# An encoder layer on one core: early feed-forward weights loaded three pairs ahead into other buffers, ten early pairs in place of nine, two of them ahead of the second normalisation

## The chip, the core and the metric

One Trainium2 chip, one core of it. TensorE (PE in the profile) multiplies matrices, with a row of its own for loading the stationary operand (PEld); VectorE (DVE), ScalarE (ACT) and GpSimd (POOL) do the element-wise work; SyncE (SP) issues most transfers. Each engine takes its instructions strictly in the order in which they were written into its queue. The metric is the device time of one execution in microseconds (us), lower is better. A measurement of this kernel is the median of several runs.

## The reference, cut to what matters

One layer over 1024 tokens of width 1024, in float32, with an input normalisation, three kinds of attention, and a feed-forward part of width 4096:

```
x    = layer_norm(x, ln_in_g, ln_in_b)
proj = x @ w_in                                  # heads A, B and C
mix  = concat(A(proj), B(proj), C(proj)) @ w_out
x    = layer_norm(alpha * x + mix, ln_mix_g, ln_mix_b)
hdn  = relu(x @ w_ff1)
x    = layer_norm(alpha * x + (hdn * hdn) @ w_ff2, ln_ff_g, ln_ff_b)
```

## The kernel before, in words

Every matrix product is made of float32 operands split into a high and a low part (a cast on ACT, then a subtraction on DVE; `split`, lines 825 and 826), and three matmuls for each pair of blocks. The two feed-forward products go through a scheme with seven products for a 2 x 2 block product (Strassen and Winograd), numbered m = 1 to 7.

**The stretch of the change** is the passage from the mixing to the first feed-forward product. The tokens are worked on in two halves of 512. `out_ab(t)` (line 792) multiplies the heads of token block t with w_out and adds the result to a running sum; `out_ab(7)` is the last. `ln_mix_half(0)` normalises token blocks 0 to 3 while the last blocks of the attention are still under way; its four pieces make the operands `xo[1]` and `xo[2]`, which are all that the products m = 1 and m = 2 need. `ln_mix_half(1)` needs `out_ab(7)`. It has four pieces too, and each makes, for one k, the operands of m = 6, 7, 5, 4 and 3: eight transposes (line 872), two activations (line 873), four differences, five splits.

**Early pairs.** The columns of w_ff1 are taken in 16 pairs of 128-column blocks, j = 0 to 15. For the first `N_EARLY` = 9 of them, m = 1 and m = 2 are done ahead of the main loop, so that TensorE has something to do while the second half is being normalised. An early pair costs one load of 512 KB (`w1_early`, line 917), two splits of two halves each, 24 matmuls of 512 columns into the PSUM tiles `psS` (line 953), a copy and a sum, a squared relu, and two stores to DRAM (`dd`, `hd`), from which the main loop reads them back. The load goes into the buffer `raw`, of which there is one, so the load of pair j + 1 can begin only when both halves of pair j have been split. `EARLY_LN` = 1 of these pairs stands ahead of `ln_mix_half(1)` in the program; the other eight stand behind its pieces, two to each piece, and their matmuls are queued behind the last transpose that was written before that piece (`after`).

**The main loop** goes through the remaining (j, m), five steps (m = 6, 7, 5, 4, 3) for an early pair and seven for another, with operands prepared five steps ahead by `w1_prep` (line 924). It loads the pair's whole 1 MB of w_ff1 into a buffer `w1r` of the tag `tab`, of which there are two. During the mixing the two `tab` buffers hold two of w_out's blocks (`hd`; `load_wout(0)` and `load_wout(1)`). The second feed-forward product follows.

Operands live in *pages* (36 buffers of 4 KB a partition, tag `pg`), given out in the program's order. A planner decides the order of instructions on each engine ahead of time, by the program's order, by priorities (`high_priority`), by its own estimate of times, and by `issue_after`, which queues what a block writes for an instruction's engine behind that instruction. Once decided, the order doesn't change on the chip.

Of the kernel before, what the change touches and what calls it, by code (L numbers as in the profile page):

```python
# [10 lines left out]
F32 = mybir.dt.float32  # L11
# [6 lines left out]
P = 128  # L18
# [35 lines left out]
LN_MIX_AT, LN_MIX_PER = 64, 2  # L54


N_EARLY, EARLY_LN = 9, 1
NORM_FIRST = 120
AHEAD, AHEAD2 = 5, 4
ROWS_AT, C_AT, LAST_STEPS = 28, 6, 8  # L60
# [17 lines left out]
def encoder_kernel(ctx: ExitStack, tc: tile.TileContext, A: dict, out: bass.AP):  # L78
    nc = tc.nc

    sb = ctx.enter_context(tc.tile_pool(name="sb", bufs=1))
# [5 lines left out]
    def nm(p):  # L87
        cnt[0] += 1
        return f"{p}_{cnt[0]}"

    def page(shape, dt=F32):
        return sb.tile(shape, dt, tag="pg", bufs=N_PG, name=nm("pg"))
# [16 lines left out]
    def ps_mm():  # L109
        return ps.tile([P, 512], F32, tag="mm", bufs=NM, name=nm("psm"))  # L110
# [13 lines left out]
    def load(out, in_):  # L124
        last_load[0] = nc.sync.dma_start(out=out, in_=in_)
# [6 lines left out]
    def half_sl(h):  # L132
        return slice(h * 512, h * 512 + 512)
# [4 lines left out]
    def mm3(o, pairs):  # L138

        n = 3 * len(pairs)  # L140
        i = 0
        for (ah, al, bh, bl) in pairs:
            for a, b in ((ah, bh), (ah, bl), (al, bh)):
                nc.tensor.matmul(o, a, b, start=(i == 0), stop=(i == n - 1))  # L144
                i += 1

# [14 lines left out]
    def w_cols(w, c0, n, k0=0, nk=8):  # L163
        return w[k0 * P:(k0 + nk) * P, c0:c0 + n].rearrange("(k p) c -> p k c", p=P)
# [162 lines left out]
    def mm_feat(w, half):  # L327
        pm = ps_mm()
        mm3(pm, [(w[0][:, k, :], w[1][:, k, :], xT[half][k][:, 0, :], xT[half][k][:, 1, :]) for k in range(8)])
        return pm  # L330
# [56 lines left out]
    def proj_tok(t, ws, dest, pm):  # L387
        xt = xT[t // 4]
        sl = slice((t % 4) * P, (t % 4) * P + P)
        mm3(pm[:, 0:256], [(xt[k][:, 0, sl], xt[k][:, 1, sl], ws[k // 4][0][:, k % 4, :], ws[k // 4][1][:, k % 4, :])  # L390
                           for k in range(8)])
        n = 4 // len(dest)
        for j, d in enumerate(dest):
            pv = pm[:, 64 * n * j:64 * n * (j + 1)].rearrange("p (h d) -> p h d", h=n)
            nc.scalar.copy(out=d[:, :, 0:64], in_=pv)
            sub(d[:, :, 64:128], pv, f32(d[:, :, 0:64]))
# [370 lines left out]
    w_out = A["w_out"]  # L767

    w_o = {}

    def load_wout(c, paged):
        dest = None
        if c < 2:
            dest = hd_tab()
        elif paged:
            dest = page([P, D], F32R), page([P, D], F32R)
        w_o[c] = split_w(w_out[c * P:(c + 1) * P, :], [P, D], dest, page([P, D]) if paged else None, pool=True)

    def heads_of(t, n):
        return [o[:, t * P:(t + 1) * P] for o in o_ca[n]]  # L780

    def out_c(t):

        for nh in range(2):
            pm = ps_mm()
            sl = half_sl(nh)
            mm3(pm, [(*heads_of(t, n), w_o[6 + n][0][:, sl], w_o[6 + n][1][:, sl]) for n in range(2)])
            a_t = evb([P, 512])
            nc.scalar.copy(out=a_t, in_=pm)
            nc.gpsimd.dma_start(out=y1[t][:, sl], in_=a_t, accum_op=ALU.add)  # L790

    def out_ab(t, ob):

        a_t = page([P, D])
        load(out=a_t, in_=y1[t])
        for nh in range(2):
            pm = ps_mm()
            sl = half_sl(nh)
            mm3(pm, [(*heads_of(t, 2 + n), w_o[n][0][:, sl], w_o[n][1][:, sl]) for n in range(2)]
                + [(ob[:, 0, n], ob[:, 1, n], w_o[2 + n][0][:, sl], w_o[2 + n][1][:, sl]) for n in range(4)])  # L800
            nc.vector.tensor_tensor(out=a_t[:, sl], in0=a_t[:, sl], in1=pm, op=ALU.add)
        return a_t
# [6 lines left out]
    w_ff1, w_ff2 = A["w_ff1"], A["w_ff2"]  # L809
# [7 lines left out]
    def tab8(shape, name):  # L817
        return sb.tile(shape, F32, tag="tab", bufs=2, name=nm(name))
# [4 lines left out]
    def split(pg, x):  # L823

        nc.scalar.copy(out=pg[:, 0], in_=x)  # L825
        last_split[0] = nc.vector.tensor_tensor(out=pg[:, 1], in0=x, in1=f32(pg[:, 0]), op=ALU.subtract)  # L826
# [86 lines left out]
    def w1_split(j, m, x):  # L913
        w1op[j, m] = page([P, 2, 4, P], F32R)
        split(w1op[j, m], x)

    def w1_early(j):

        w = sb.tile([P, 8, P], F32, tag="raw", bufs=1, name=nm("w1e"))
        load(out=w, in_=w_cols(w_ff1, 256 * j, P))  # L920
        for c in range(2):
            w1_split(j, 1 + c, w[:, 4 * c:4 * c + 4])

    def w1_prep(j, m):

# [305 lines left out]
    for n in range(64 + B_VALUES):  # L1231
# [20 lines left out]
        for _ in range(2):  # L1252
            m = a_done[0]
            if m < 16 and n > 31 + C_VALUES and n >= 32 + m + A_VALUES:
                h, b = divmod(m, 4)
# [7 lines left out]
        if m >= 0:  # L1263
            t, g = divmod(m, 2)
            if g == 0:
                oTb[t] = page([P, 2, 4, P], F32R)
            b_values(t, g, b_rt.pop(m), b_vs, oTb[t])
            if g == 1:
                with tc.high_priority(offset=-(OUT_OFF if t < NT - 1 else 0)):
                    fa[t] = out_ab(t, oTb.pop(t))  # L1270
# [11 lines left out]

    early = range(N_EARLY)

    def ahead(j, after=None):
        if j + 1 < N_EARLY:
            w1_early(j + 1)
        with (tc.issue_after(after.ins) if after else ExitStack()):
            ff1(j, 1, True)
            ff1(j, 2, True)  # L1290

    w1_early(0)
    for j in early[:EARLY_LN]:
        ahead(j)
    pieces = ln_mix_half(1)
    rest = list(early[EARLY_LN:])
    for k in range(4):
        after = last_tr[0]
        pieces[k]()
        for j in rest[k * len(rest) // 4:(k + 1) * len(rest) // 4]:  # L1300
            ahead(j, after)
# [138 lines left out]
```

## Time and profile before

| | |
|---|---|
| median of three runs | 1206.79 us (1206.04 to 1209.1) |
| profiled execution | 1206.19 us, of which 1204.4 us are the span of the trace |
| mean granted TensorE clock over the span | 0.986 |
| PE, PEld busy | 1143.8 us, 946.1 us of the span |
| DVE, ACT, POOL busy | 956.2 us, 641.3 us, 413.4 us |

Times in the rows are microseconds from the start of the span. A matmul's record is longer than its pace, since matmuls are pipelined: one of 512 columns is recorded with 0.39 us. The chain of waits gives the pace, since there each piece ends where the next begins. An idle time stands in brackets with what ended it.

### The profile page before, as it was taken

The numbers are of one execution on the slowest core, as the hardware profiler recorded it, in microseconds if no ns is written. First come the engines' busy times: TensorE is split into PE (matmuls) and PEld (weight loads), VectorE is DVE, ScalarE is ACT, GpSimd is POOL, SyncE is SP. The second block draws the span as 40 slices with busy tenths as digits, with TensorE's granted clock in tenths as the row PEclk, the third lists the DMA queues.
The fourth block names the chain that finished last, engine by engine and source line by source line (L and its number), as shares of the span: only waits on it lengthen the run. The fifth ranks groups of instructions, "written<-read, shape, count | busy, mean of one in ns | idle before, by whom it ended". The sixth has DMA issues, their size and how long they took to land.

```text
span 1204.4 us, 17122 instructions
## 1 busy us (share of the span) xinstructions
PE 1143.8 (95%) x5642; PEld 946.1 (79%) x5642; DVE 956.2 (79%) x1858; ACT 641.3 (53%) x1253; POOL 413.4 (34%) x367
## 2 busy tenths in 40 slices
PE   4999999999988989998799999999999999999997
PEld 3788789878877868876568888888888888888885
DVE  8556999998666598876569989988884997787985
ACT  4534667666556877755564544545553444444530
POOL 4775656775666865320011222221210000000201
PEclk8999999999999999999899999999999999999998
DMA  8566844364769962224355678665599655355631
GB/s 275 190 235 186 280 135 144 114 161 135 233 195 282 190 144 88 63 79 149 100 171 199 229 258 283 237 236 199 174 345 367 225 182 183 95 175 186 227 123 70
DMA packets 138000, 227.15 MB, mean 189 GB/s; under 512 B 11820, under 2 KB 75212, under 8 KB 137912
## 3 DMA queue, kind: packets, MB, share of 16 engines
q1 hardware_dynamic: 122472, 177.55, 46.9%
q0 software_dynamic: 15440, 48.51, 11.7%
q8 instruction: 45, 0.74, 0.3%
q14 instruction: 43, 0.35, 0.1%
HBM read 156.49 MB, written 77.34 MB: 194 GB/s over the span
## 4 chain that ended last, share of the span: by engine, by line
PE 72%; DVE 8%; ACT 4%; issue 3%; DMA 3%; POOL 1%; SPq 0%; DVEq 0%; ACTq 0%; POOLq 0%
PE psm L144 13%; PE psS L1083 11%; PE psS L953 8%; PE pst L953 7%; PE psm L953 7%; PE psm L1083 5%; PE pst L1083 5%; PE pspv L1083 4%; DMA w1e<-in_w_ff 2%; PE pspv L514 2%; PE pst L499 2%; PE psS L470 2%; DVE pg L473 1%; DVE pg L130 1%; DVE pg L826 1%
## 5 line engine op out<-in xcount | busy, mean ns | idle before, releaser
L144 PE MATMUL psm<-pg,whi 128*128 128x512 f32 x448 | 152.7, 406 | 2.1 <-DVE pg L245 1.8
L953 PE MATMUL psS<-pg,pg 128*128 128x512 f32 x576 | 139.9, 396 | 8.2 <-ACT pg L825 5.2
L217 POOL TENSOR_TENSOR bnve<-bnve,pw 128x1 f32<-128x1 f32 x24 | 22.5, 939 | 357.5 <-DVE bnve L216 355.3
L1083 PE MATMUL psS<-pg,pg 128*128 128x512 f32 x576 | 140.4, 389 | 0.0
L953 PEld LDWEIGHTS psS<-pg,pg 128*128 128x128 f32 x576 | 108.2, 190 | 35.0 <-ACT pg L825 8.4
L1083 PEld LDWEIGHTS psS<-pg,pg 128*128 128x128 f32 x576 | 108.1, 188 | 22.4
L825 ACT CAST pg<-hr 128x512 fp32r<-128x512 f32 x112 | 69.3, 619 | 97.5 <-PE pst L1083 39.5
L477 ACT ACTIVATE pg<-pg,cst 128x1024 f32<-128x1024 f32 x64 | 73.8, 1154 | 51.6 <-DVE cst L473 48.6
L144 PEld LDWEIGHTS psm<-pg,whi 128*128 128x128 f32 x448 | 83.7, 191 | 21.7 <-DVE pg L245 2.2
L144 PE MATMUL psm<-pg,wlo 128*128 128x512 f32 x224 | 89.3, 399 | 0.8 <-POOL wlo L160 0.8
L953 PE MATMUL psm<-pg,pg 128*128 128x512 f32 x384 | 89.8, 389 | 0.0
L953 PE MATMUL pst<-pg,pg 128*128 128x512 f32 x384 | 89.6, 389 | 0.0
L826 DVE TENSOR_TENSOR pg<-hr,pg 128x512 fp32r<-128x512 f32 x112 | 76.7, 685 | 13.6 <-ACT pg L825 13.4
L953 PEld LDWEIGHTS pst<-pg,pg 128*128 128x128 f32 x384 | 72.1, 188 | 15.0
L953 PEld LDWEIGHTS psm<-pg,pg 128*128 128x128 f32 x384 | 72.1, 188 | 15.0
L130 DVE TENSOR_TENSOR pg<-pst,pg 128x512 fp32r<-128x512 f32 (+2 forms) x112 | 65.0, 589 | 22.2 <-ACT pg L639 8.1
L484 POOL TENSOR_TENSOR pg<-pg,cst 128x704 f32<-128x704 f32 x32 | 49.2, 1536 | 80.1 <-DVE cst L481 57.7
L1083 PE MATMUL psm<-pg,pg 128*128 128x512 f32 x288 | 74.2, 389 | 0.0
L1083 PE MATMUL pst<-pg,pg 128*128 128x512 f32 x288 | 74.2, 389 | 0.0
L144 PE MATMUL psm<-whi,pg 128*128 128x256 f32 (+1 forms) x256 | 72.4, 349 | 1.0 <-DVE pg L130 0.7
L961 POOL DMA_DIRECT2D hd<-evb x80 | 43.2, 540 | 85.6 <-DVE evb L821 80.9
L964 ACT ACTIVATE h<-h 128x512 f32<-128x512 f32 x55 | 34.5, 631 | 71.1 <-DVE h L821 71.0
(208 smaller groups left out, 2769.2 us busy)
## 6 DMA issues: line engine op xcount, KB each, us to landing
hr<-hd SPq DMA_DIRECT2D x28, 1024.0 KB, 5.7
hd<-evb POOLq DMA_DIRECT2D x80, 256.0 KB, 4.1
w1r<-in_w_ff SPq DMA_DIRECT2D x16, 1024.0 KB, 5.4
evb<-in_w_ff SPq DMA_DIRECT2D x64, 256.0 KB, 3.6
qk<-evb SPq DMA_DIRECT2D x52, 256.0 KB, 4.2
y<-pg POOLq DMA_DIRECT2D x24, 512.0 KB, 4.7
pg<-y SPq DMA_DIRECT2D x24, 512.0 KB, 9.2
pg<-in_w_ff SPq DMA_DIRECT2D x32, 256.0 KB, 6.0
```

The costliest lines, as they stand in the source:

```text
L130: nc.vector.tensor_tensor(out=o, in0=a, in1=b, op=ALU.subtract)
L144: nc.tensor.matmul(o, a, b, start=(i == 0), stop=(i == n - 1))
L470: last_mm[0] = nc.tensor.matmul(sc, q[:, m, (i % 2) * P:(i % 2) * P + P], kst[h][kh][:, m, :], start=True, stop=True)
L477: nc.scalar.activation(out=rt, in_=rt, func=AF.Exp, scale=-1.0, bias=sm[:, m:m + 1], accum_out=sm[:, 2 + m:3 + m])
L484: nc.gpsimd.tensor_tensor(out=R[1][:, a], in0=R[1][:, a], in1=sm[:, 6:7].broadcast_to([P, C_POOL]), op=ALU.mult)
L499: nc.tensor.transpose(pt[:, kb * P:(kb + 1) * P], src[:, c0:c0 + P], ident)
L825: nc.scalar.copy(out=pg[:, 0], in_=x)
L826: last_split[0] = nc.vector.tensor_tensor(out=pg[:, 1], in0=x, in1=f32(pg[:, 0]), op=ALU.subtract)
L953: nc.tensor.matmul(o, w[:, e, k], xo[m][k][:, f], start=(n == 0), stop=(n == 11))
L961: nc.gpsimd.dma_start(out=hd_d[m - 1, j], in_=x)
L964: nc.scalar.activation(out=dst, in_=dst, func=AF.Relu)
L1083: nc.tensor.matmul(o, h[:, e, sl], w[:, f], start=(k == 0 and n == 0), stop=(k == 15 and n == 2))
```

## The change

The loading of an early pair's weights is taken out of `w1_early` and becomes `w1_early_load`. It runs three pairs ahead: pairs 0, 1 and 2 are loaded before the first split, and pair j + 3 is loaded when pair j is worked on. Pair 0 still goes into `raw`, pairs 1 and 2 into a page each, and pairs 3 to 9 into the two `tab` buffers, from which the mixing's w_out blocks have gone and into which `w1_prep` loads afterwards. There are ten early pairs, not nine, and two of them, not one, ahead of `ln_mix_half(1)`. The matmuls of these two are now queued behind the last matmul of `out_ab(7)` (`last_ab`, which `mm3` returns); before, the one such pair had no such tie.

```diff
--- before.py
+++ after.py
@@ -54,7 +54,7 @@
 LN_MIX_AT, LN_MIX_PER = 64, 2
 
 
-N_EARLY, EARLY_LN = 9, 1
+N_EARLY, EARLY_LN = 10, 2
 NORM_FIRST = 120
 AHEAD, AHEAD2 = 5, 4
 ROWS_AT, C_AT, LAST_STEPS = 28, 6, 8
@@ -141,8 +141,9 @@
         i = 0
         for (ah, al, bh, bl) in pairs:
             for a, b in ((ah, bh), (ah, bl), (al, bh)):
-                nc.tensor.matmul(o, a, b, start=(i == 0), stop=(i == n - 1))
+                mm = nc.tensor.matmul(o, a, b, start=(i == 0), stop=(i == n - 1))
                 i += 1
+        return mm
 
 
 
@@ -767,6 +768,7 @@
     w_out = A["w_out"]
 
     w_o = {}
+    last_ab = [None]
 
     def load_wout(c, paged):
         dest = None
@@ -796,7 +798,7 @@
         for nh in range(2):
             pm = ps_mm()
             sl = half_sl(nh)
-            mm3(pm, [(*heads_of(t, 2 + n), w_o[n][0][:, sl], w_o[n][1][:, sl]) for n in range(2)]
+            last_ab[0] = mm3(pm, [(*heads_of(t, 2 + n), w_o[n][0][:, sl], w_o[n][1][:, sl]) for n in range(2)]
                 + [(ob[:, 0, n], ob[:, 1, n], w_o[2 + n][0][:, sl], w_o[2 + n][1][:, sl]) for n in range(4)])
             nc.vector.tensor_tensor(out=a_t[:, sl], in0=a_t[:, sl], in1=pm, op=ALU.add)
         return a_t
@@ -914,12 +916,24 @@
         w1op[j, m] = page([P, 2, 4, P], F32R)
         split(w1op[j, m], x)
 
+    w1e = {}
+
+    def w1_early_load(j):
+
+        if j >= N_EARLY:
+            return
+        if j == 0:
+            w1e[j] = sb.tile([P, 8, P], F32, tag="raw", bufs=1, name=nm("w1e"))
+        else:
+            w1e[j] = page([P, 8, P]) if j < 3 else tab8([P, 8, P], "w1e")
+        load(out=w1e[j], in_=w_cols(w_ff1, 256 * j, P))
+
     def w1_early(j):
 
-        w = sb.tile([P, 8, P], F32, tag="raw", bufs=1, name=nm("w1e"))
-        load(out=w, in_=w_cols(w_ff1, 256 * j, P))
-        for c in range(2):
-            w1_split(j, 1 + c, w[:, 4 * c:4 * c + 4])
+        if j < N_EARLY:
+            w = w1e.pop(j)
+            for c in range(2):
+                w1_split(j, 1 + c, w[:, 4 * c:4 * c + 4])
 
     def w1_prep(j, m):
 
@@ -1282,16 +1296,19 @@
 
     early = range(N_EARLY)
 
-    def ahead(j, after=None):
-        if j + 1 < N_EARLY:
-            w1_early(j + 1)
-        with (tc.issue_after(after.ins) if after else ExitStack()):
+    def ahead(j, after):
+
+        w1_early_load(j + 3)
+        w1_early(j + 1)
+        with tc.issue_after(after.ins):
             ff1(j, 1, True)
             ff1(j, 2, True)
 
+    for j in range(3):
+        w1_early_load(j)
     w1_early(0)
     for j in early[:EARLY_LN]:
-        ahead(j)
+        ahead(j, last_ab[0])
     pieces = ln_mix_half(1)
     rest = list(early[EARLY_LN:])
     for k in range(4):
```

## Rows read from the trace of the kernel before

**Rows 1.** Windows: busy time (count) of each engine, granted clock, DMA share, GB/s.

```profile
558.19:629.42 71.23, 58.43 (x244) 44.29 (x242) 41.50 (x70) 39.34 (x71) 9.24 (x17) 0.95 0.49 157
...
570.00:580.00 10.00, 5.98 (x19) 4.81 (x20) 4.75 (x9) 4.00 (x6) 1.70 (x3) 0.66 0.43 142
...
630.00:1100.00 470.00, 470.00 (x2075) 389.17 (x2075) 394.49 (x628) 219.09 (x384) 61.48 (x114) 1.00 0.65 224
```

**Rows 2.** The chain that ended last, 559 to 643 us: start, duration, what.

```profile
559.65 6.11 DMA w1e<-in_w_ff
...
576.67 6.00 PE psS L953 x19
...
582.68 0.45 PE pst L872 x4
...
588.83 0.60 DVE evb L130
...
624.37 4.36 DMA w1e<-in_w_ff
...
637.95 5.44 PE psm L953 x24
```

**Rows 3.** TensorE in order of time: start, duration, work, [idle before, releaser].

```profile
559.58 2.00 PE L144 MATMUL psm<-pg,pg 128*128 128x512 f32 x8
...
561.41 4.02 PE L953 MATMUL psS<-pg,pg 128*128 128x512 f32 x17
...
565.26 0.40 PE L144 MATMUL psm<-whi,pg 128*128 128x512 f32 x1
...
568.97 0.40 PE L144 MATMUL psm<-whi,pg 128*128 128x512 f32 x1
...
573.36 0.69 PE L872 MATMUL pst<-ident,pg 128*128 128x128 f32 x2 [3.99 <-DVE pg L862]
...
574.71 1.97 PE L872 MATMUL pst<-ident,pg 128*128 128x128 f32 x8 [0.66 <-ACT pg L873]
...
587.15 1.25 PE L953 MATMUL psS<-pg,pg 128*128 128x512 f32 x4 [2.00 <-ACT pg L825]
...
590.09 4.87 PE L953 MATMUL psS<-pg,pg 128*128 128x512 f32 x20 [1.08 <-DVE pg L826]
...
629.42 8.53 PE L953 MATMUL psS<-pg,pg 128*128 128x512 f32 x36 [1.15 <-ACT pg L825]
```

**Rows 4.** DVE in order of time, same columns.

```profile
560.69 0.87 DVE L130 TENSOR_TENSOR pg<-evb,pg 64x256 fp32r<-64x256 f32 x2 [0.47 <-ACT pg L762]
...
567.71 0.68 DVE L801 TENSOR_TENSOR pg<-pg,psm 128x512 f32<-128x512 f32 x1
...
631.33 0.69 DVE L821 TENSOR_TENSOR w1t<-w1r 128x512 f32<-128x512 f32 x1
...
634.13 0.69 DVE L826 TENSOR_TENSOR pg<-w1t,pg 128x512 fp32r<-128x512 f32 x1 [1.39 <-ACT pg L825]
```

**Rows 5.** ACT in order of time, same columns.

```profile
583.89 2.17 ACT L825 CAST pg<-evb 128x512 fp32r<-128x512 f32 x4
...
586.48 1.14 ACT L825 CAST pg<-w1e 128x512 fp32r<-128x512 f32 x2
```

**Rows 6.** Waits of ACT from 569.3 to 629.5 us: total, times, longest.

```profile
ACT pg L825 <- DMA w1e<-in_w_ff: 10.8, 6, 5.5
```

**Rows 7.** SP's queue in order of time, same columns as rows 3.

```profile
552.95 1.08 SPq L125 DMA_DIRECT2D w1r<-in_w_ff  x2
...
554.20 1.26 SPq L125 DMA_DIRECT2D pg<-y  x1
```

**Rows 8.** DMA issues, 400 to 660 us: count, KB each, us to landing.

```profile
w1r<-in_w_ff SPq DMA_DIRECT2D x5, 1024.0 KB, 5.4
...
w1e<-in_w_ff SPq DMA_DIRECT2D x9, 512.0 KB, 4.0
...
pg<-y SPq DMA_DIRECT2D x8, 512.0 KB, 9.5
```

## The prediction, made blind

> **What bounds the kernel now.** I read the windows first, to find where TensorE is not full; then the chain of waits and TensorE in order of time through that place; then DVE, ACT and SP there, to see what each gap waits for.
>
> From 630 us on TensorE is busy without a gap (470.00 of 470.00 us, clock 1.00) [rows 1]. So whatever makes the main loop begin earlier brings the end earlier by as much. From 558.19 to 629.42 it is not full. The pace is 24 matmuls in 5.44 us, 0.227 us each, and four transposes in 0.45 us [rows 2]. The stretch holds 24 matmuls of `out_ab(7)`, 192 of the first eight early pairs (by the code; the block of 36 at 629.42 is the ninth pair's 24 and the main loop's first 12) and 32 transposes: 216 x 0.227 + 32 x 0.11 = 52.5 us in 71.2 us. **18.7 us are lost there.** In four places [rows 2, 3]:
> - 568.97 to 576.67: 4.0 us without any work until the last token block is normalised, then transposes that wait on ACT. Some 6 us.
> - 576.67 to 582.68: 19 matmuls take 6.00 us where 4.3 are due. TensorE's clock was granted at 0.66 of 2.4 GHz over 570 to 580 [rows 1], so part of it ran at 1.2 GHz, after that idle stretch. 1.7 us.
> - 582.68 to 590.09: 9 matmuls and 16 transposes (3.8 us) in 7.4 us. The gap of 2.0 us ends with a split on ACT, and the split of the early weights (586.48) stands behind four casts of the normalisation (583.89) [rows 5]. Its load was not late; its place in ACT's order was. 3.6 us.
> - 590.09 to 629.42: 140 matmuls, 31.7 us, in 39.3 us. 7.6 us. The chain shows the load of the early weights five times (first 6.11, last 4.36 us) [rows 2], and ACT's casts wait 10.8 us for these loads [rows 6]. One buffer, a load of 4.0 us [rows 8] and a split make a cycle longer than the 5.44 us of matmuls that it feeds.
>
> By PE's busy time alone (58.43 of 71.23 [rows 1]) only 12.8 us would be lost. The Trainium skill says in "Perfetto Trace Analysis", section "Identifying the Most-Contended Engine", that matmul busy time is a poor measure, since matmuls are pipelined, and that the busy share of weight loads is a better one. By that measure PEld's 44.29 us at the 0.828 of the full stretch (389.17 of 470.00) are 53.5 us of work and 17.7 us lost. The trace agrees: a count by pace gives 18.7. By busy time the sum below would end about 6 us higher.
>
> **The change part by part.**
>
> *Pairs 0 and 1 behind `out_ab(7)`.* Now 17 matmuls of pair 0 run between the two parts of `out_ab(7)` (561.41 to 565.26), more are mixed into the second part, and its last starts at 568.97 [rows 3]. Without them: 12 matmuls from 558.19 to 560.9; the operand of the other 12 is ready at 560.69 + 0.87 = 561.56 [rows 4]; 12 x 0.227 = 2.7, end at 564.3. If the second part starts no earlier than now (565.26), it ends at 568.0. I take 564.3, as the operand allows it; bounds 0 and 3.7 us later.
>
> *What the normalisation's gap then holds.* From the last matmul to the first dependent transpose there are 4.4 us (568.97 to 573.36). Two pairs are 10.9 us of work and cover it with 6.5 us to spare, so the gap and the slow clock behind it are gone: cost 0, and 6 + 1.7 us if that cover fails.
>
> *Ten pairs with loads ahead.* From 564.3: 240 x 0.227 + 32 x 0.11 = 58.0, so the main loop could begin at 622.3. Now it begins at 629.42 + 5.44 = 634.86, with one pair (5.44 us) more left in it. Ceiling: 634.86 + 5.44 - 622.3 = **18.0 us**.
>
> *What is kept of the stalls.* The 16 transposes ahead of pair 2 go through two banks that ACT empties: 573.36 to 576.67 is 3.3 us for at most 1.8 of work. Minus 1.5 (bounds 0 and 2.2). ACT's order: pair 2's split is now written ahead of the second normalisation, the later ones not. I keep half of 3.6: minus 1.8 (bounds 0 and 3.6). Load waits: a load is due two pairs after its issue, 10.9 us against 4.0 alone and, for several together, the 9.5 us of the y load issued right behind two large ones [rows 7, 8]: 0 (bound 2).
>
> *The main loop's weights.* `w1r` for pairs 0 and 1 is now loaded at 552.95 [rows 7], long before its use at 631.33 [rows 4]. The early pairs take those buffers, so it comes after the split of pair 8. Then 5.4 us of load [rows 8] and 3.5 us of preparation (631.33 to 634.13 + 0.69) are 8.9 us, against 10.9 us of matmuls of pairs 8 and 9 if that split is done as pair 8 starts. Minus 1 (bounds 0 and 3).
>
> *At no cost.* SP: pairs 3 and 4 take the place of the two `w1r` loads in its queue. Behind these stands the sum's load (554.20); 9.5 us later it is there at 563.7, the first sum could start at about 563, and a microsecond there stays under the 6.5 us of cover. The tenth pair adds one load, two stores and two loads back, and SP and POOL are mostly idle here. DVE and ACT have 41.50 and 39.34 us of work in the 71.2 us [rows 1]; with the tenth pair's share (three DVE instructions of 0.60 us [rows 2], two casts and three activations on ACT of about as much each) that fits into 64. Its splits leave the main loop, where DVE has 394.49 of 470 us busy and TensorE stays full. Two pages more are taken, shortly before `out_ab(7)` gives back eight (four of heads, four of weights); without that cover the two loads start 5 us later and still come before pair 1 is due at 569.7.
>
> Sum: 18.0 - 1.5 - 1.8 - 1.0 = 13.7 us. The profiled execution took 1206.19 us, 0.6 below the median: 1206.19 - 13.7 = **1192.5 us**.
>
> **The rivals.** Three microseconds and a half (0.3%) are what a measurement here tells from no change.
> - *Order, not loads, sets the pace* (0.20). Only the last part's 7.6 us come back, since transposes and splits stay as tangled in the planned order as now: 1198.6, within 1197 to 1203. For it: DVE waits on ACT and ACT on transposes between 577 and 587. Against: two pairs written and split ahead of the tangle.
> - *One wait for another* (0.10). The loads now wait for pages or for `tab` buffers, and what the early pairs gain the main loop loses on `w1r`: 7.6 + 6 gained at most, 3.7 lost at `out_ab(7)`, up to 8.9 at `w1r` if the split of pair 8 is as late as pair 9. That leaves a gain of 1.0, 1205.2, within 1203 to 1208. Against: 10.9 us of matmuls between.
> - *Slower* (0.13). Pair 0 is no longer there to fill TensorE while the last attention block is finished. The fill is 3.85 us (561.41 to 565.26), and a gap of that length was followed by 1.7 us of slow clock: 5.6 us. If ACT's place in the order, and not the loads, is what holds the pairs, so that less than 5.6 us come back, the kernel is slower, up to 1211.8. Against: the operand is there at 561.56, and ACT waited 10.8 us on loads.
>
> **How the numbers follow.** Forecast 0.57, by itself 1188 (all 18.0 us) to 1198 (stalls at their bounds, 2.2 + 3.6 + 2 + 2). With the first rival and part of the second, 1188 to 1204 holds eight in ten. Faster: 0.57 + 0.20 + 0.03 = 0.80; the same 0.07; slower 0.13 with the slow edge of the second rival in it.
>
> **What would show it.** Right: no wait of ACT on `w1e` loads, no `w1e` in the chain, the clock near 1.00 through 570 to 580, `out_ab(7)` ending near 564, the main loop's first `psS` matmuls near 626, `w1r` issued about 610. Wrong, if TensorE is empty between 561 and 565 for long, if the first main step waits for `w1r`, or if the gaps before early matmuls stay and name ACT's casts with loads long landed: then the order, and not the loads, was the pace.

## The result, and the profile after

The changed kernel took 1192.43 us (median of four runs, 1191.89 to 1196.56), the kernel before 1206.41 us over its four runs. The ratio is 0.9893, 95% interval 0.986 to 0.9926: 0.7 to 1.4% faster, clear of the 0.3% within which two times can't be told apart here. 1192.5 us were forecast. The profiled execution has a span of 1190.4 us where it was 1204.4.

The windows of the kernel after, with the columns of [rows 1]. The first stretch goes from the same place, the 12 matmuls of `out_ab(7)` on pages, to the main loop's first step:

```profile
557.89:626.53 68.64, 65.85 (x292) 53.23 (x291) 46.75 (x78) 43.96 (x80) 11.41 (x21) 0.98 0.59 191
...
570.00:580.00 10.00, 9.70 (x48) 7.61 (x47) 4.59 (x7) 6.16 (x10) 2.74 (x5) 1.00 0.42 157
...
586.00:590.00 4.00, 3.92 (x12) 3.06 (x13) 4.00 (x8) 4.00 (x9) 0.00 (x0) 0.57 0.00 0
...
630.00:1080.00 450.00, 450.00 (x1987) 372.63 (x1986) 381.60 (x608) 209.34 (x365) 59.86 (x111) 1.00 0.67 230
```

TensorE is still full from 630 us on, so the whole difference lies ahead of it. Before, that stretch held nine pairs and lasted from 558.19 to 634.86, 76.7 us; now it holds ten and lasts 68.6. With 5.44 us for the tenth pair that is 13.5 us, and the span is 14.0 us shorter; the rest is 0.3 us at the beginning of the stretch and 0.2 behind it. The slow clock of 570 to 580 is gone (1.00 for 0.66), but there is a new and shorter one at 586 to 590 (0.57).

TensorE in order of time, to be set against [rows 3]:

```profile
557.89 2.90 PE L144 MATMUL psm<-pg,pg 128*128 128x512 f32 x12
560.84 0.51 PE L144 MATMUL psm<-whi,pg 128*128 128x512 f32 x1
...
563.72 10.62 PE L967 MATMUL psS<-pg,pg 128*128 128x512 f32 x46
574.17 0.38 PE L874 MATMUL pst<-ident,pg 128*128 128x128 f32 x2
...
575.31 1.32 PE L874 MATMUL pst<-ident,pg 128*128 128x128 f32 x8 [0.29 <-ACT pg L875]
576.39 5.28 PE L967 MATMUL psS<-pg,pg 128*128 128x512 f32 x22
581.51 0.60 PE L874 MATMUL pst<-ident,pg 128*128 128x128 f32 x4
...
586.08 2.61 PE L967 MATMUL psS<-pg,pg 128*128 128x512 f32 x6 [2.45 <-ACT pg L827]
...
589.20 40.05 PE L967 MATMUL psS<-pg,pg 128*128 128x512 f32 x174
```

The second part of `out_ab(7)` starts at 560.84, not 565.26, and its end is followed without a gap by 46 matmuls of pairs 0 and 1. The 4.0 us of idle time are gone. The 174 matmuls at 589.20, six pairs and more, have no gap between them; before, nearly the same work (176 matmuls) was in eight pieces, from the one at 590.09 to the one at 629.42 [rows 3], each behind a wait. What is left is one idle time of 2.45 us, for a split on ACT, with six matmuls in 2.61 us behind it (1.36 are due).

The chain of waits holds no load of early weights any more; five stood in it (the first and the last are in [rows 2]):

```profile
563.88 10.46 PE psS L967 x46
...
576.64 5.04 PE psS L967 x22
...
586.08 2.61 PE psS L967 x6
588.69 0.85 PE pst L874 x4
589.54 39.70 PE psS L967 x174
629.25 5.44 PE psm L967 x24
```

DVE, ACT and SP in order of time:

```profile
564.51 1.29 DVE L828 TENSOR_TENSOR pg<-pg,pg 128x512 fp32r<-128x512 f32 x2 [3.25 <-ACT pg L827]
565.72 0.68 DVE L803 TENSOR_TENSOR pg<-pg,psm 128x512 f32<-128x512 f32 x1
566.32 0.68 DVE L828 TENSOR_TENSOR pg<-pg,pg 128x512 fp32r<-128x512 f32 x1
...
570.58 0.81 DVE L864 TENSOR_SCALAR pg<-pg,bnmv,bnve 128x1024 f32<-128x1024 f32 x1 [0.76 <-POOL bnve L218]
...
615.13 0.69 DVE L823 TENSOR_TENSOR w1t<-w1r 128x512 f32<-128x512 f32 x1 [1.24 <-DMA w1r<-in_w_ff]
...
617.24 0.69 DVE L828 TENSOR_TENSOR pg<-w1t,pg 128x512 fp32r<-128x512 f32 x1
```

```profile
563.86 1.14 ACT L827 CAST pg<-pg 128x512 fp32r<-128x512 f32 x2 [3.07 <-DMA pg<-in_w_ff]
...
582.15 0.78 ACT L875 ACTIVATE pg<-pst,ln_mix_cols 128x512 f32<-128x512 f32 x1 [2.12 <-PE pst L874]
582.83 2.17 ACT L827 CAST pg<-evb 128x512 fp32r<-128x512 f32 x4
...
585.41 2.18 ACT L827 CAST pg<-w1e 128x512 fp32r<-128x512 f32 x4
```

```profile
553.91 1.06 SPq L125 DMA_DIRECT2D pg<-y  x1
555.06 2.10 SPq L125 DMA_DIRECT2D pg<-in_w_ff  x2
...
607.90 6.38 SPq L125 DMA_DIRECT2D w1r<-in_w_ff  x2
```

Three things are to be seen. The split that TensorE waits for (585.41) is that of pair 3: it stands behind four casts of the normalisation (582.83), as pair 2's did before [rows 5]. These stand behind an activation that waits for transposes, and on TensorE the transposes (581.51) stand behind pair 2's 22 matmuls. The second normalisation was not made much earlier: `out_ab(7)` ends 5.5 us sooner (its last matmul starts at 563.48, before at 568.97 [rows 3]), but the splits of pairs 1 and 2, whose loads went out behind the sum's own (555.06) and kept ACT waiting 3.07 us, stand ahead of the sums on DVE, and the last block is normalised at 570.58 where it was 572.49 (below). And the main loop's first weights, loaded from 607.90 on, are prepared at 617.24 + 0.69 = 617.9, 8.6 us before their use. In the kernel before, the last block's normalisation on DVE:

```profile
572.49 0.81 DVE L862 TENSOR_SCALAR pg<-pg,bnmv,bnve 128x1024 f32<-128x1024 f32 x1 [1.03 <-POOL bnve L217]
```

### The profile page after: what moved, and what is told of

It is laid out like the page before. It is cut to its first block, busy times and chain, and to the rows that moved or that the text cites. A ratio compares the mean times of both kernels' runs of the same rounds, so it can differ in the third digit from the quotient of the medians.

```text
span 1190.4 us, 17144 instructions
## 1 busy us (share of the span) xinstructions
PE 1141.3 (96%) x5642; PEld 947.8 (80%) x5642; DVE 953.1 (80%) x1858; ACT 642.1 (54%) x1253; POOL 414.6 (35%) x368
## 4 chain that ended last, share of the span: by engine, by line
PE 79%; DVE 5%; ACT 3%; issue 2%; POOL 0%; DMA 0%; SPq 0%; DVEq 0%; ACTq 0%; POOLq 0%
PE psm L144 15%; PE psS L967 11%; PE psS L1097 11%; PE pst L967 7%; PE psm L967 7%; PE pst L1097 5%; PE psm L1097 5%; PE pspv L1097 4%; PE pspv L515 2%; PE psS L471 2%; PE pst L500 2%; PE pspv L754 1%; DVE pg L130 1%; PE pspv L652 1%; PE psS L725 1%
## 5 line engine op out<-in xcount | busy, mean ns | idle before, releaser
L1097 PE MATMUL psS<-pg,pg 128*128 128x512 f32 x576 | 140.5, 389 | 0.0
L967 PE MATMUL psS<-pg,pg 128*128 128x512 f32 x576 | 136.2, 393 | 2.4 <-ACT pg L827 2.4
L478 ACT ACTIVATE pg<-pg,cst 128x1024 f32<-128x1024 f32 x64 | 73.9, 1154 | 51.4 <-DVE cst L474 48.4
L828 DVE TENSOR_TENSOR pg<-hr,pg 128x512 fp32r<-128x512 f32 x112 | 76.7, 685 | 13.0 <-ACT pg L827 12.9
L827 ACT CAST pg<-evb 128x512 fp32r<-128x512 f32 x80 | 48.6, 617 | 39.5 <-DVE evb L823 39.4
```

Of the source, the lines that this page charges most:

```text
L478: nc.scalar.activation(out=rt, in_=rt, func=AF.Exp, scale=-1.0, bias=sm[:, m:m + 1], accum_out=sm[:, 2 + m:3 + m])
L967: nc.tensor.matmul(o, w[:, e, k], xo[m][k][:, f], start=(n == 0), stop=(n == 11))
L1097: nc.tensor.matmul(o, h[:, e, sl], w[:, f], start=(k == 0 and n == 0), stop=(k == 15 and n == 2))
```

## The experiments

Two theories stood at the beginning. Mine: two separate losses, the gap behind `out_ab(7)` (filled by the second pair ahead of the norm) and the waits on loads (ended by the early loads), some 7 us each. The rivals: the order alone, or the loads alone, does it all. To compare kernels apart from what varies ahead of the stretch (in the twelve profiled executions it began between 557.5 and 561.1 us), I also give its length in the trace: from the 12 matmuls of `out_ab(7)` to the main loop's second step, m = 7, with 5.44 us taken off for each pair above nine. Before: 558.19 to 637.95, 79.8 us. Changed kernel: 557.89 to 629.25, less 5.44: 65.9 us.

**Loads alone.** Against the changed kernel:

```diff
-N_EARLY, EARLY_LN = 10, 2
+N_EARLY, EARLY_LN = 9, 1
...
-        with tc.issue_after(after.ins):
+        with (tc.issue_after(after.ins) if after else ExitStack()):
...
-        ahead(j, last_ab[0])
+        ahead(j, None)
```

> The changed kernel with the early loads and their buffers alone: nine early pairs, one ahead of the second norm, not tied to out_ab(7). Two separate sources (my theory): the waits on loads behind 590 us are gone, 7.6 us back, while the idle stretch after out_ab(7) stays (6 us and 1.7 us of slow clock), so 1199, within 1197 to 1201. If the loads are everything: 1192 to 1194. If the order of the pairs is everything: 1204 or more.

1197.78 us, ratio 0.9934 (0.9913 to 0.9954). The stretch is 561.08 to 633.65, 72.6 us, 7.2 less than before. (The profiled execution was the slowest of the six, 1201.92 us, and of all twelve its stretch began latest; the length leaves that out.) TensorE in order of time:

```profile
576.43 0.69 PE L874 MATMUL pst<-ident,pg 128*128 128x128 f32 x2 [4.22 <-DVE pg L864]
...
590.12 1.25 PE L967 MATMUL psS<-pg,pg 128*128 128x512 f32 x4 [1.94 <-ACT pg L827]
...
593.06 20.77 PE L967 MATMUL psS<-pg,pg 128*128 128x512 f32 x90 [0.50 <-DVE pg L828]
614.31 19.33 PE L967 MATMUL psS<-pg,pg 128*128 128x512 f32 x84 [0.48 <-ACT ev L995]
```

The gap behind `out_ab(7)` is as long as before (4.22 for 3.99), the one for the split too (1.94 for 2.00), and behind 590 only two half microseconds are left. The early loads take away the waits on loads and nothing else.

**Order alone.** The kernel before with the pairs' order of the changed one:

```diff
-N_EARLY, EARLY_LN = 9, 1
+N_EARLY, EARLY_LN = 10, 2
...
-        ahead(j)
+        ahead(j, last_ab[0])
```

> The kernel before with ten early pairs, two of them ahead of the second norm and tied behind out_ab(7), but with one buffer for the early weights, each load behind the splits of the pair before. My theory: the idle stretch after out_ab(7) is filled (7.7 us back), the pairs from the third on again go at the pace of load and split, about 6.7 us each where 5.44 are due, for one pair more than before: 1199, within 1196 to 1203. If the order is everything: 1192 to 1194. If the loads are everything: 1205 or more.

1200.31 us, ratio 0.995 (0.9931 to 0.9969). The stretch is 559.08 to 638.43, less 5.44: 73.9 us, 5.9 less than before. `out_ab(7)` is followed at once by 46 matmuls, and behind 590 us the chain of waits is again one of loads; four of its pieces, and below them ACT's waits for early weights from 569.3 to 630.5:

```profile
591.80 4.08 DMA w1e<-in_w_ff
...
605.66 4.52 DMA w1e<-in_w_ff
...
618.79 4.07 DMA w1e<-in_w_ff
624.86 4.37 DMA w1e<-in_w_ff
```

```profile
ACT pg L827 <- DMA w1e<-in_w_ff: 15.9, 7, 5.5
```

15.9 us of waits on loads, where the changed kernel has 2.6 on `w1e` and 3.5 on the two pages in its whole stretch from 557.89 on. By the traces, one execution of each kernel, the two parts are worth 7.2 and 5.9 us, together 13.1 of 13.8. Neither rival holds.

**Nine pairs.** The changed kernel with `N_EARLY, EARLY_LN = 9, 2`.

> The changed kernel with nine early pairs in place of ten. TensorE is full from 590 us on in the changed kernel, so by my theory the tenth pair is worth nothing: 1191.5 to 1193.5. If the tenth pair covers the second norm's splits or the late loads of the main loop's weights, up to its 5.4 us are lost: 1194 to 1198, with a gap before the main loop's first step.

1195.12 us, ratio 0.9918 (0.9895 to 0.9941): a miss, 2.7 us slower than the changed kernel, in the range that I had given to the rival but without the rival's gap at the main loop. By the times alone it could not be told from the changed kernel, since the intervals of the two ratios overlap; but its stretch is 68.2 us, 2.3 more. A window of TensorE alone in the nine-pair kernel (busy time, count, clock):

```profile
588.00:594.00 6.00, 5.70 (x13) 0.50 0.44 130
```

In the nine-pair kernel the order around the gap is a little other (four matmuls, four transposes, another wait of 0.60 us), and TensorE then runs at 1.2 GHz until 594, 13 matmuls in 6 us, where the changed kernel is at 0.57 only from 586 to 590 (above) and at 2.4 GHz again behind that. So most of what the tenth pair is worth here is a shorter slow stretch behind a gap that both have; why the order there is other with nine pairs the runs don't show.

**No tie.** The changed kernel with the pairs ahead of the norm not tied to `out_ab(7)` (the last two edits of the loads-only kernel).

> The changed kernel without the tie of the first two pairs to the last matmul of out_ab(7). My theory: pair 0, and perhaps pair 1, mix with out_ab(7) as before, which ends 5 to 10 us later; what is left of them behind it covers the 4.4 us of the norm's chain or not. 1192.5 if one pair's matmuls are left, 1198 to 1200 if none is, with the slow clock behind the gap. If the tie does nothing: 1191.5 to 1193.5 with out_ab(7) ending near 564.

1192.6 us, ratio 0.9887 (0.9868 to 0.9906), the same as with the tie; the stretch is 558.34 to 629.94, less 5.44: 66.2 us. TensorE in order of time:

```profile
561.08 4.92 PE L967 MATMUL psS<-pg,pg 128*128 128x512 f32 x21
565.84 0.40 PE L144 MATMUL psm<-whi,pg 128*128 128x512 f32 x1
...
569.32 5.63 PE L967 MATMUL psS<-pg,pg 128*128 128x512 f32 x24
574.79 0.38 PE L874 MATMUL pst<-ident,pg 128*128 128x128 f32 x2
```

`out_ab(7)` ends 5.6 us later than with the tie (its last matmul starts at 569.09, there at 563.48), much as before the change (568.97), and pair 1's 24 matmuls behind it fill the norm's gap by themselves. What counts is that a second pair is there, not where it is tied.

**Three ahead.** The changed kernel with `N_EARLY, EARLY_LN = 10, 3`.

> The changed kernel with three of the ten early pairs ahead of the second norm and tied behind out_ab(7), not two; the fourth pair's split is thereby also written ahead of the norm. What is left in the changed kernel is one gap of 2.45 us near 584, in which the fourth pair waits for a split that stands behind the norm's casts on ACT, and 1.3 us of slow clock behind it. If it is the place of that split in the order: 1188 to 1190. If the norm's own chain now comes too late for the main loop: the gap moves to the main loop's first steps, 1192 to 1196.

1195.6 us, ratio 0.9926 (0.9913 to 0.9939): the 1188 to 1190 that I had hoped for were missed, and the time lies in the range of the alternative, but not for the reason given there. The gap did not go, it moved one pair on; and a second wait stands before the main loop's second step:

```profile
591.00 1.64 PE L967 MATMUL psS<-pg,pg 128*128 128x512 f32 x4 [2.45 <-ACT pg L827]
...
632.00 5.13 PE L967 MATMUL psm<-pg,pg 128*128 128x512 f32 x14 [1.89 <-ACT pg L827]
```

The second wait is not for the norm, whose last transposes start at 592.44 and whose last casts end at 614.9. It ends with a cast of the main loop's own weights. DVE had to make their difference first, and waited 2.43 us for the store of an early pair's result (`hd` from `ha`) to land; in the program `ha` and `w1s` take turns in the two buffers of one tag (`mask`):

```profile
630.60 0.69 DVE L130 TENSOR_TENSOR w1s<-w1r 128x512 f32<-128x512 f32 x1 [2.43 <-DMA hd<-ha]
```

```profile
631.33 0.62 ACT L827 CAST pg<-w1s 128x512 fp32r<-128x512 f32 x1 [1.83 <-DVE w1s L130]
```

The first wait is that of the changed kernel, one pair later. With splits one pair ahead, the first pair behind the norm has its successor's split behind the norm's first casts, with one pair ahead of the norm (before), with two (changed) and with three.

**Splits two pairs ahead.** The changed kernel, loads and pairs as they are:

```diff
         w1_early_load(j + 3)
-        w1_early(j + 1)
+        w1_early(j + 2)
...
     w1_early(0)
+    w1_early(1)
```

> The changed kernel with each early pair's split written two pairs ahead, not one; loads, pairs and their places as in the changed kernel. If the split's place in ACT's order is the last stall: the gap near 584 and the slow clock behind it are gone, 3.7 us back, 1188 to 1190. If ACT's casts were late for want of transposes, whatever they wait for: the next split or a bank of PSUM takes its place, 1191 to 1193.5.

**1188.36 us** (1187.77 to 1189.0), ratio 0.9861 (0.9845 to 0.9876): faster than the kernel before by 1.2 to 1.6%, and its highest run is below the changed kernel's lowest. The kernel before, run along with each, took 1204.77 us with this one and 1206.41 with the changed one, and the intervals of the two ratios overlap a little, so the gain over the changed kernel rests mainly on the trace. The stretch is 557.49 to 625.28, less 5.44: 62.4 us, 3.6 less than in the changed kernel. TensorE:

```profile
582.22 0.60 PE L874 MATMUL pst<-ident,pg 128*128 128x128 f32 x4
582.58 4.82 PE L967 MATMUL psS<-pg,pg 128*128 128x512 f32 x20
...
589.65 35.20 PE L967 MATMUL psS<-pg,pg 128*128 128x512 f32 x154
625.28 5.80 PE L967 MATMUL psm<-pg,pg 128*128 128x512 f32 x24 [0.42 <-ACT pg L827]
```

On ACT pair 3's split now comes ahead of the norm, 19 us earlier than the 585.41 of the changed kernel:

```profile
566.36 1.14 ACT L827 CAST pg<-w1e 128x512 fp32r<-128x512 f32 x2
```

Pair 3's matmuls follow the transposes without a wait, and the clock is 1.00 over 570 to 630. The split's place in ACT's queue was the last large stall. Two short waits stay, 0.76 us before the second group of transposes and the 0.42 us at 625.28, which goes back to the store of an early pair's result as in the kernel with three pairs ahead.

**Before with one load.** In the kernel before, the load in `w1_early` is made for pair 0 alone and all nine pairs split that buffer.

> The kernel before with one load of early weights in place of nine: all nine pairs split the first pair's weights out of the one buffer, so the early products of pairs 1 to 8 are left out in favour of copies of pair 0's. Order of the pairs as before. If the waits on loads behind 590 us are what the early loads brought back in the loads-only kernel, this gives the same: 1198, within 1196 to 1200, with the gap behind out_ab(7) in place. If taking the loads out gives much less (1203 or more), the buffers' order and not the loads made the difference there; if much more (1194 or less), the loads also hold up the norm.

1197.52 us, ratio 0.9939 (0.9926 to 0.9951), as forecast, and as the loads-only kernel. The gaps of 3.68 us behind `out_ab(7)` and 2.00 us at the split are there; from 589.51 on 174 matmuls follow each other without one:

```profile
589.51 39.74 PE L957 MATMUL psS<-pg,pg 128*128 128x512 f32 x174 [0.50 <-DVE pg L826]
```

So the loads themselves were the wait, not the buffers' order. Its stretch is 2 us shorter than that of the loads-only kernel (558.72 to 629.25, 70.5 us), a difference that the medians do not show.

**Nine pairs, splits two ahead.** The splits-two-ahead kernel with `N_EARLY, EARLY_LN = 9, 2`.

> Nine early pairs with each split two pairs ahead. The nine-pair kernel lost 2.7 us against ten, with the clock at half speed from 587 to 594 us behind the gap, where the ten-pair kernel has it so from 586 to 590. If the tenth pair was worth something only through the length of that slow stretch, nine and ten pairs are equal once the gap is gone: within 1 us of the ten-pair kernel with splits two ahead, 1188 to 1190. If the tenth pair has a worth of its own: 2 to 3 us slower than that one.

1191.52 us, ratio 0.9886 (0.9873 to 0.99): 3.2 us slower than ten pairs. The stretch is 559.22 to 622.96, 63.7 us, 1.4 more, of which 1.15 are a wait of TensorE for a copy on ACT that stands behind casts waiting 2.44 us for a load of early weights:

```profile
609.18 13.48 PE L967 MATMUL psS<-pg,pg 128*128 128x512 f32 x58 [1.15 <-ACT ev L995]
```

```profile
606.99 1.14 ACT L827 CAST pg<-w1e 128x512 fp32r<-128x512 f32 x2 [2.44 <-DMA w1e<-in_w_ff]
```

With splits two ahead the loads are only one pair ahead of them. So nine pairs are slower without the late gap too; why this load is late with nine pairs and none costs TensorE anything with ten, the runs don't show. What makes up the other 1.8 us of the medians the trace doesn't show; the stretch of this profiled execution began 1.7 us later, which by the spread named above may be chance.

**Eleven pairs, splits two ahead**, and **no tie, splits two ahead.** Both start from the splits-two-ahead kernel: the first has `N_EARLY` = 11, the second leaves out the tie by the same two edits as above.

> Splits two pairs ahead, eleven early pairs. With ten, TensorE is full from 576 us on but for 0.4 us, so an eleventh pair should be worth nothing: 1187.5 to 1189.5. If more early pairs have a worth of their own (ten against nine gave 3.2 us, of which the traces show 1.4 as gaps): 1185 to 1187. If it delays the main loop's weights: 1190 or more.

> Splits two pairs ahead, ten early pairs, without the tie of the first two to out_ab(7). In the changed kernel the tie was worth nothing (1192.6 against 1192.4), since one pair's matmuls behind out_ab(7) cover the norm's chain either way. If that holds without the later gap too: within 1 us of 1188.4. If the tie buys an earlier norm that the later gap had hidden: 1 to 4 us slower, with the norm's transposes and the main loop later by as much.

1189.19 us, ratio 0.9843 (0.9817 to 0.9869), and 1189.03 us, ratio 0.9854 (0.9826 to 0.9882). Both are the same as the splits-two-ahead kernel within what can be told, and so are the stretches: 61.9 us (559.18 to 631.96, less 10.88) and 61.6 us (558.66 to 625.73, less 5.44) for 62.4. In neither does TensorE wait from the second group of transposes (577.03, 576.24) to the main loop. With TensorE full there, more early pairs or another place of the first two bring nothing.

## Why the prediction was right, point by point

- **Where the time is lost** held: nothing changed behind the main loop's start but by its earlier beginning. The count was a little off. In the stretch there are 26 transposes, not 32 (the other six lie ahead of it; in the trace after they run in two groups of three at 555.95 and 557.33), so 19.3 us were lost and not 18.7, and the ceiling was 18.7 us, not 18.0.
- **`out_ab(7)`**: 564.3 was forecast from a start at 558.19, 6.1 us; 563.88 - 557.89 = 6.0 was measured.
- **The norm's gap** cost nothing, as forecast, but the cover was tighter. From the start of the last matmul to the end of the last normalisation it took 7.9 us (563.48 to 571.39), not 4.4 and a little, because on DVE the splits of pairs 1 and 2 stand ahead of the sums and among them. Of the cover 2.8 us were left (to the first transpose at 574.17), not 6.5. I had looked for what the two loads delay on SP and not for what their late landing delays on DVE.
- **Stalls kept**: 4.3 us were forecast in three terms, 5.3 were there (563.88 to 626.53 less 240 x 0.227 and 26 x 0.11), and the main loop's first step came at 626.5 where 626 was forecast. The transposes' banks: 0.8 for 1.5. ACT's order: 4.1 (the gap of 2.45, and behind it 1.25 on six matmuls and 0.4 on four transposes at the slow clock) for 1.8, above the bound of 3.6 that I gave. The main loop's weights: 0 for 1.0. So the mechanism held for the banks and for ACT's order, ACT's order was sized too small, the stall at the main loop's weights was not there, and the errors of the terms nearly cancelled. That 1192.5 met 1192.43 is in part luck: by the terms as measured the sum would be 18.7 - 5.3 = 13.4 for 13.7.
- **Load waits** at 0: behind 589.54 there are 0.2 us (39.70 for 174 matmuls). The loads-only and the one-load kernels show the same from both sides. My sign for it was too strict, though: ACT still waited for early weights, 2.6 us on `w1e` and 3.5 us on the two pages, but TensorE had work enough meanwhile.
- **The rivals.** *Order, not loads* gave 1198.6, within 1197 to 1203, since only the waits on loads would come back. The measured time lies below that, and the order-only kernel shows what it left out, 5.9 us from the order of the pairs. Yet it names rightly what stayed, and one of my signs of being wrong was there in part: a gap of 2.45 us that names ACT's cast, for weights whose load went out at 552.66 and whose split came at 585.41. *One wait for another*: `w1r` came 8.6 us early. *Slower*: TensorE was not empty between 561 and 565, since the operand was there, as argued.

## What to carry to other kernels

When a load feeds an engine through another engine's in-order queue, moving the load ahead is half of it: the instruction that uses the loaded data must also stand ahead, in its queue, of whatever will be late. Price a filler by the gap that it has to cover and check the cover once more for work that the change itself puts into the chain. When a gap moves instead of going (three ahead), count the distance between producer and consumer in the queue, not the number of fillers.

## What the runs showed that I had not expected

The slow clock behind a gap is not in proportion to it. In the kernel before, an idle time of 3.99 us [rows 3] came with half speed (a granted clock of 0.50, read half a microsecond at a time) from 573.2 to 580 us; with 4.22 us in the loads-only kernel and 3.68 us in the one-load kernel it lasted as long, some 6.8 us. In the changed kernel a gap of 2.45 us was followed by some 3.4 us of it, and so it was in the order-only, the no-tie and the three-ahead kernel (2.44, 2.45 and 2.45 us). In the nine-pair kernel the same 2.45 us, with four matmuls and four transposes and 0.60 us more idle time behind it, were followed by 6.8 us, to 594 us, while matmuls already followed each other from 588.30 on. Gaps of 2.00 us in the kernel before and in the one-load kernel and of 1.94 us in the loads-only kernel were followed by none (0.99 over 580 to 590 before, where the first 0.1 us still belong to the slow stretch ahead of it; 1.00 in all windows from 580 to 600 in the one-load kernel, and from 586 to 600 in the loads-only one). So the price of a gap of 2.0 to 2.5 us here lay between nothing and 3.0 us beside the gap itself (the 152 matmuls from 588.30 on took 37.49 us in the nine-pair kernel, where 34.5 were due). What decided between 3.4 and 6.8 us behind the same 2.45 us the runs don't show.
